# The opening of an encoder kernel, arranged by quarters of the channels

## The chip, the cores and the metric

The kernel runs on one core of a Trainium2 chip. The metric is the device time of one execution in microseconds, the median of several runs. The core has five engines with a queue each: TensorE (PE, with its weight loads as PEld), VectorE (DVE), ScalarE (ACT), GpSimd (POOL) and SyncE (SP), which here issues nearly all DMA transfers.

## What is computed

A two-layer encoder (1024 channels) runs over two sequences: a prompt of 256 tokens and a sample of 512. Each layer normalizes, scales and shifts by a vector that depends on the sequence, mixes the tokens (layer 0 by a gated recurrence in both directions, layer 1 by windowed attention), and then runs a feed-forward part with a short convolution. The change lies in the first microseconds of layer 0:

```python
mod = jax.nn.silu(c) @ adaln_w[l] + adaln_b[l]            # 1024 x 6144
sh1, sc1, g1, sh2, sc2, g2 = jnp.split(mod, 6, axis=-1)
h = rmsnorm(x, norm_g[l, 0]) * (1 + sc1) + sh1
proj = h @ w_in                                           # queries, keys, values, o, gates
q, k, v, o = ...
gates = proj[..., 4096:] + b_gate                         # input and forget gate, both directions
b = cumsum(log_sigmoid(forget)); m = running max(input - b)
```

The gates feed scans over time (cumulative sums and running maxima), whose results weigh the products of queries and keys.

## The kernel before

**Layout.** Channels lie on the 128 partitions, in KC = 8 blocks (called channels c = 0 to 7 here), tokens along the free dimension: 768 columns, the prompt at 0 to 255 and the sample at 256 to 767. RANGES names the sample's first half (r0), its second half (r1) and the prompt (r2). Products run in a split form: an operand is its rounded high part plus a low part (`hh` and `hl` for activations, `whi` and `wlo` for weights), and a product is three matmuls: high by high, high by low, low by high. One *tile* of a projection is 128 output columns by all eight channels, so 24 matmuls for the sample and 24 for the prompt.

**The opening.** `first` (L1728) loads x by ranges and starts `adaln` (L418), which computes shift and scale, the first 2048 columns of the modulation matrix `adaln_w`. It loads sixteen pieces of 128 rows by 1024 columns (512 KB each, the last in two halves), in the order of the rows, and multiplies each by the activated condition `silc` (32 columns, two in use) into four column groups of one PSUM bank. A result is complete only when the last row block is in. Then ACT and DVE copy the bank, PE turns it by 128-column blocks, and DVE adds the bias and forms the gains (1 + scale) * g. Between the loads the helper `warm` (L414) issues plain fp32 matmuls of ones. The two sample ranges are normalized meanwhile (`Norm`, L91: squares on ACT, sums on POOL and PE, a power on POOL, a spread of the factor over partitions on PE), and `scaled` multiplies x by the factor.

`mlstm` (L665) then loads the first two weight halves (`U_MIN`, the queries of head 0), the prompt's x and the rest of the constants, and calls `opening` (L908). There the order of PE, ACT and DVE is written out by hand (`manual_schedule`). Three tiles run: the gates, and the two halves of the queries of head 0. r0 is modulated channel by channel (`made`, `cast`, `lower`) and multiplied, then r1, then the prompt, whose factor comes from a `Norm` of its own. `ahead` (L300) loads and splits the next weight, the first tile of the keys (`U_MIN + 1`, half 0), and is noted as `opened`. The three sinks take the results away.

**Behind it.** The fourth tile, the first of the keys, runs in the loop at L754, then the second, then the values (`gemmN`). `decay` (L696) forms the logarithms and scans on DVE, writes the running maxima to DRAM (L713), and `maxima` (L727) reads them back, spread over partitions. `columns` turns the gates. The rest of the modulation is filled in later: `adaln_g` on PE, `adaln_v` on DVE (one reduction over 1024 columns per vector, L539), the first of them behind `opened`.

**What sets the order.** Outside hand-ordered blocks a list scheduler orders each engine's instructions by a simulated time; on the chip every queue runs in that order. Buffers come from pools with a fixed number of slots: six `slab`, five `raw` (loads of 512 KB), three each of `whi` and `wlo`, four PSUM banks each of `ps` and `pa`. A load waits on SP until its slot is free.

Of the kernel before, what the change touches and what calls it, by code (L numbers as in the profile page):

```python
# [11 lines left out]
F32 = mybir.dt.float32  # L12
# [4 lines left out]
P = 128  # L17
D = 1024
# [33 lines left out]
SOON = AB + 96  # L52
# [129 lines left out]
class Net:  # L182
# [235 lines left out]
    def adaln(self, l, th):  # L418
        nc = self.nc
        hold = None  # L420

        def fetch(i):
            nonlocal hold
            k, h = divmod(i, 2)
            c0 = th * 2048 + h * 1024
            src = self.io["adaln_w"][l, k * P : (k + 1) * P, c0 : c0 + 1024]
            if k < 2:
                return self.raw(src)
            z = (i - 4) % 3
            if z == 0:  # L430
                hold = self.slab([P, 3, 1024])
            for part in parts(i):
                cut = lambda a: a.rearrange("p (g m) -> p g m", g=2)[:, :, part] if len(parts(i)) > 1 else a
                nc.sync.dma_start(cut(hold[:, z]), cut(src))
            return hold[:, z]

        def parts(i):
            return [slice(0, 256), slice(256, 512)] if i == 2 * KC - 1 else [slice(0, 512)]

        ps, pt = self.ps(), self.ps()  # L440
        for i in range(2 * KC):
            k, h = divmod(i, 2)
            cur = fetch(i)
            for part in parts(i):
                for g in range(2):
                    r0 = 32 * (2 * h + g)
                    last = nc.tensor.matmul(
                        ps[r0 : r0 + 32, part], self.silc[:, k, :], cur[:, g * 512 : (g + 1) * 512][:, part],
                        start=k == 0, stop=k == KC - 1, skip_group_check=True,
                    )  # L450
            if h and k > 2:
                with self.tc.issue_after(last.ins):
                    self.warm(pt, 6 if k < KC - 2 else 2 if k < KC - 1 else 1)
            if i < 2 * KC - 1 and h:
                yield
        sb = [self.tmp([P, 256]) for _ in range(2)]
        nc.vector.tensor_copy(sb[0], ps[:, :256])
        nc.scalar.copy(sb[1], ps[:, 256:])
        for b in range(4):
            self.turned = nc.tensor.transpose(  # L460
                pt[:, b * P : (b + 1) * P], sb[b // 2][:, (b % 2) * P : (b % 2 + 1) * P], self.ident
            )
        src = pt.rearrange("p (b g s) -> p g b s", b=4, g=4)[:, :, :, 0:2]
        dst = self.mod[l][:, th * 16 : (th + 1) * 16, :].rearrange("p (g b) s -> p g b s", g=4)
        ab = self.cst(AB + 48 * l + 16 * th, 16).rearrange("p (g b) -> p g b", g=4)
        for s in range(2):
            nc.vector.tensor_tensor(dst[:, :, :, s], src[:, :, :, s], ab, ALU.add)
            if th == 0:
                nc.vector.scalar_tensor_tensor(
                    self.gain[l][0][:, :, s],  # L470
                    self.mod[l][:, 8:16, s],
                    1.0,
                    self.cst(NG + 16 * l, 8),
                    ALU.add,
                    ALU.mult,
                )
        yield

# [42 lines left out]
    def adaln_v(self, columns, pool):  # L521
# [4 lines left out]
        nc.sync.dma_start(row, self.crow.to_broadcast([P, 2, 1024]))  # L526
# [41 lines left out]

    def scaled(self, x, pr, rng):
        for c in range(KC):  # L570
            self.nc.vector.tensor_tensor(x(c), x(c), pr, ALU.mult)
        return ()
# [92 lines left out]
    def mlstm(self, pool, gw, xt):  # L665
# [8 lines left out]
        nc.vector.memset(B[0:G], 0.0)  # L674
# [16 lines left out]
        nc.sync.dma_start(self.kct[:, P:], io["kc"][:, P : 3 * P])  # L691
        nc.sync.dma_start(self.cstt[:, SOON:], io["cst"][:, SOON:])
        self.opening(xt, gw, raws, (gates, keep(qt0, 0, 0), keep(qt0, 0, 1)))
# [53 lines left out]
        for h in range(4):  # L747
# [5 lines left out]
            qk = [] if h else [qt0]  # L753
            todo = ((i, c, w) for i in range(0 if h else 1, 2) for c, w in self.halves(U_MIN + 3 * h + i))  # L754
# [153 lines left out]
    def opening(self, xt, gw, raws, sinks):  # L908

        nc = self.nc  # L910
# [3 lines left out]
        hi, lo = ([self.stg.tile([P, 1024], R, tag=t, name=self.nm(t), bufs=3) for _ in range(2)] for t in ("whi", "wlo"))  # L914
        w = [[t.rearrange("p (k m) -> p k m", k=KC) for t in part] for part in ([gw[0], *hi], [gw[1], *lo])]
        low = lambda i: tt(lo[i], raws[i], hi[i].bitcast(F32), ALU.subtract)
        high = lambda i: nc.scalar.copy(hi[i], raws[i])
# [3 lines left out]
        def mm(rng, i, z, a, c, stop=False):  # L921
            c0, c1, q = rng
            s0 = SEQS[q][0]
            o = bank[i, q][:, c0 - s0 : c1 - s0]
            self.mm(o, w[z][i][:, c], both[a][:, c, c0:c1], (i, c0) not in begun, stop)
            begun.add((i, c0))

        def three(rng, i, c):
            for z, a in ((0, 0), (1, 0), (0, 1)):
                mm(rng, i, z, a, c, c == KC - 1 and a == 1)  # L930
# [7 lines left out]
        r0, r1, r2 = RANGES  # L938
# [3 lines left out]
        shift = lambda c, q: self.mod[0][:, c, q : q + 1]  # L942
        gain = lambda c, q: self.gain[0][0][:, c, q : q + 1]

        def sample(rng):
            c0, c1, q = rng
            x = lambda c: xt[c // 4][:, c % 4, c0:c1]
            h = lambda c: self.hh[:, c, c0:c1]

            def made(c):  # L950
                if c % 2:
                    act(x(c), x(c), AF.Identity, scale=gain(c, q), bias=shift(c, q))
                else:
                    nc.vector.tensor_scalar(x(c), x(c), gain(c, q), shift(c, q), ALU.mult, ALU.add)

            cast = lambda c: nc.scalar.copy(h(c), x(c))  # L956
            lower = lambda c: tt(self.hl[:, c, c0:c1], x(c), h(c).bitcast(F32), ALU.subtract)
            return made, cast, lower

        def operands(rng, *between):  # L960
            made, cast, lower = sample(rng)
            made(0)
            made(1)
            made(2)
            cast(0)
            cast(1)
            for c in range(0, KC, 2):
                lower(c)
                if c + 2 < KC:
                    cast(c + 2)  # L970
                lower(c + 1)
                if c + 4 < KC:
                    made(c + 4)
                if c + 2 < KC:
                    made(c + 3)
                    cast(c + 3)
                if c < 2 * len(between):
                    between[c // 2]()

        squares = lambda c0: [norm.square(c) for c in range(c0, c0 + 4)]  # L980

        with self.tc.manual_schedule(engines={eng.PE, eng.Activation, eng.DVE}):
            for i in range(3):
                bank[i, 0] = self.ps()
            with self.tc.issue_after(self.turned.ins):
                self.warm(bank[0, 0], 5)
            high(0)
            operands(r0)
            high(1)
            low(0)  # L990
            low(1)
            squares(0)
            for c in range(0, KC, 2):
                for k in (c, c + 1):
                    three(r0, 0, k)
                for k in (c, c + 1):
                    mm(r0, 1, 0, 0, k)
                    mm(r0, 1, 0, 1, k)
            for c in range(KC):
                mm(r0, 2, 0, 0, c)  # L1000
                mm(r0, 2, 0, 1, c)
            for i in (1, 2):
                for c in range(KC):
                    mm(r0, i, 1, 0, c, c == KC - 1)

            operands(r1, lambda: squares(4))
            for c in range(0, KC, 2):
                if c == 4:
                    next(factor)
                if c == 6:  # L1010
                    next(factor, None)
                for i in range(3):
                    for k in (c, c + 1):
                        three(r1, i, k)
# [4 lines left out]
            def first(c):  # L1019
                t = self.tmp([P, c1 - c0])  # L1020
                stt(t, xt[c // 4][:, c % 4, c0:c1], gain(c, q), got[r2], ALU.mult, ALU.mult)
                act(self.hh[:, c, c0:c1], t, AF.Identity, bias=shift(c, q))
                return t
# [857 lines left out]
```

## Time and profile before

| | us |
|---|---|
| median of 3 runs (lowest to highest) | 1803.8 (1800.6 to 1807.4) |
| the profiled execution | 1803.0 |
| its span, first to last instruction | 1801.0 |
| mean granted TensorE clock over the span | 0.997 |

The profile shows one execution. A line of the timeline or of the chain gives the start and the length in us and then what ran; a line of a group gives the number of instructions, their busy time and the mean length of one in ns, and behind the second bar the idle time of the engine ahead of them and what ended it. The start of the next matmul, not the modelled end, tells what a matmul costs PE. The lines that matter stand in the prediction.

### The profile page before, as it was taken

Reading aid. Unit: us, or ns where it says so; the run is one execution under the profiler, and the core shown is the slowest. Engines: PE = TensorE matmul, PEld = TensorE weight load, DVE = VectorE, ACT = ScalarE, POOL = GpSimd, SP = SyncE. Lnnn points to the kernel's source line nnn. Section 1 sums busy time; section 2 is a strip of 40 time slices with the busy share of each in tenths; the row PEclk is TensorE's granted clock in tenths of the full one; section 3 lists DMA queues with packets and bytes.
Section 4 is the critical chain, followed back from the end, with each engine's and each line's share of the span. In section 5 each row is a group of like instructions: output and inputs, shape, how many; then the busy total and the mean of one; then the engine's idle time right before and its main releaser. Section 6 shows DMA issues by size and latency. Waiting matters only on the chain.

```text
span 1801.0 us, 28821 instructions
## 1 busy us (share of the span) xinstructions
PE 1763.2 (98%) x11140; PEld 1640.9 (91%) x11140; DVE 1390.2 (77%) x2196; ACT 898.3 (50%) x1822; POOL 511.8 (28%) x433
## 2 busy tenths in 40 slices
PE   7999999999999999999999999999999999999998
PEld 4989878989998999999999999989989999999998
DVE  4887677994899777777777867767998777777877
ACT  4545434443574444444444657665564444444443
POOL 3102010231134233333331314320244333333323
PEclk9999999999999999999999999999999999999999
DMA  9354656555212222222222321233122222222212
GB/s 359 100 168 150 202 191 221 169 180 195 80 50 71 71 70 61 69 71 71 71 71 84 110 89 45 60 101 128 47 82 71 71 71 71 71 71 71 71 36 71
DMA packets 64996, 185.07 MB, mean 103 GB/s; under 512 B 6247, under 2 KB 24839, under 8 KB 64732
## 3 DMA queue, kind: packets, MB, share of 16 engines
q1 hardware_dynamic: 64284, 182.72, 31.8%
q8 instruction: 87, 1.43, 0.3%
q10 hardware_dynamic: 576, 0.52, 0.1%
q14 instruction: 49, 0.40, 0.1%
HBM read 176.77 MB, written 6.44 MB: 102 GB/s over the span
## 4 chain that ended last, share of the span: by engine, by line
PE 84%; DVE 5%; DMA 5%; ACT 3%; issue 2%; POOL 1%; SPq 0%; POOLq 0%; DVEq 0%; ACTq 0%
PE ps L269 26%; PE pa L269 23%; PE ps L1358 11%; PE ps L1359 10%; PE ps L1361 10%; DMA raw<-in_adaln_t_dram 2%; DVE junk L539 1%; DMA raw<-in_w_dram 1%; PE pa L1197 1%; DMA slab<-in_adaln_w_dram 1%; DMA raw<-in_adaln_w_dram 1%; DVE wlo L276 1%; PE pa L1359 0%; PE pa L1358 0%; ACT whi L275 0%
## 5 line engine op out<-in xcount | busy, mean ns | idle before, releaser
L275 ACT CAST whi<-raw 128x1024 fp32r<-128x1024 f32 (+1 forms) x231 | 241.0, 1045 | 342.9 <-PE pa L269 143.8
L276 DVE TENSOR_TENSOR wlo<-raw,whi 128x1024 fp32r<-128x1024 f32 (+1 forms) x231 | 315.9, 1369 | 118.2 <-ACT whi L275 115.8
L269 PE MATMUL pa<-slab,whi 128*128 128x256 f32 (+1 forms) x1280 | 307.6, 335 | 0.0
L269 PEld LDWEIGHTS pa<-slab,whi 128*128 128x128 f32 x1280 | 222.2, 188 | 21.6 <-DVE slab L603 0.4
L603 DVE SCALAR_TENSOR_TENSOR slab<-pa,mod,slab 128x256 f32<-128x256 f32 (+1 forms) x320 | 187.2, 603 | 61.5 <-PE pa L269 61.3
L269 PE MATMUL pa<-slab,wlo 128*128 128x512 f32 (+1 forms) x640 | 205.7, 334 | 0.0
L269 PE MATMUL ps<-zh,whi 128*128 128x256 f32 (+1 forms) x560 | 187.6, 336 | 0.3 <-ACT zh L956 0.3
L269 PE MATMUL ps<-zl,whi 128*128 128x256 f32 (+1 forms) x560 | 183.9, 331 | 0.5 <-DVE zl L564 0.5
L269 PE MATMUL ps<-zh,wlo 128*128 128x256 f32 (+1 forms) x560 | 181.4, 329 | 0.2 <-DVE wlo L276 0.2
L1358 PE MATMUL ps<-zh,whi 128*128 128x384 f32 x504 | 172.5, 342 | 3.8 <-ACT nt L1429 1.9
L269 PE MATMUL ps<-slab,whi 128*128 128x384 f32 (+2 forms) x704 | 172.0, 329 | 0.9 <-DVE slab L276 0.5
L539 DVE CUSTOM_DVE_ANT_0 junk<-raw,crow,cstt 128x1024 f32<-128x1024 f32 x112 | 148.6, 1327 | 30.5 <-DMA raw<-in_adaln_t_dram 29.7
L1359 PE MATMUL ps<-zl,whi 128*128 128x384 f32 x504 | 169.9, 337 | 0.8 <-DVE zl L1315 0.8
L1361 PE MATMUL ps<-zh,wlo 128*128 128x384 f32 x504 | 169.2, 336 | 0.0
L1394 POOL TENSOR_TENSOR raw<-raw,raw 128x512 f32<-128x512 f32 x40 | 53.9, 1348 | 318.4 <-DVE wlo L276 245.6
L1610 POOL TENSOR_TENSOR slab<-slab 128x772 f32<-128x772 f32 x44 | 86.6, 1969 | 166.9 <-DVE slab L1598 149.2
L269 PEld LDWEIGHTS pa<-slab,wlo 128*128 128x128 f32 x640 | 120.4, 188 | 13.2 <-DVE wlo L276 0.4
L1597 DVE SCALAR_TENSOR_TENSOR slab<-slab,cstt,slab 128x771 f32<-128x771 f32 x88 | 105.2, 1198 | 26.5 <-ACT slab L1595 26.3
L269 PEld LDWEIGHTS ps<-slab,whi 128*128 128x128 f32 x704 | 122.5, 188 | 3.4 <-ACT whi L275 0.9
L269 PEld LDWEIGHTS ps<-zh,whi 128*128 128x128 f32 x560 | 106.5, 190 | 13.1 <-issue 3.9
L269 PEld LDWEIGHTS ps<-zl,whi 128*128 128x128 f32 x560 | 106.4, 190 | 9.6 <-DVE zl L564 0.7
L269 PE MATMUL ps<-slab,wlo 128*128 128x384 f32 (+2 forms) x352 | 114.8, 328 | 0.1
(304 smaller groups left out, 4293.3 us busy)
## 6 DMA issues: line engine op xcount, KB each, us to landing
raw<-in_w_dram SPq DMA_DIRECT2D x208, 512.0 KB, 3.8
raw<-in_adaln_t_dram SPq DMA_DIRECT2D x56, 512.0 KB, 4.4
raw<-in_adaln_w_dram SPq DMA_DIRECT2D x28, 512.0 KB, 3.9
slab<-in_x_dram SPq DMA_DIRECT2D x12, 512.0 KB, 8.8
slab<-in_adaln_w_dram SPq DMA_DIRECT2D x11, 512.0 KB, 9.2
slab<-mrows SPq DMA_DIRECT2D x8, 384.0 KB, 6.9
xs<-slab SPq DMA_DIRECT2D x6, 512.0 KB, 3.1
bt<-brow SPq DMA_DIRECT2D x16, 192.0 KB, 3.1
```

What stands on the lines that cost most here:

```text
L269: self.nc.tensor.matmul(out, lhsT, rhs, start=start, stop=stop)
L275: nc.scalar.copy(hi, src)
L276: return nc.vector.tensor_tensor(lo, src, hi.bitcast(F32), ALU.subtract)
L539: nc.vector.tensor_tensor_reduce(out=junk, in0=w, in1=row[:, s], scale=1.0, scalar=self.cst(AB + 48 * l + j), op0=ALU.mult, op1=ALU.add, a ...
L603: return self.nc.vector.scalar_tensor_tensor(x, o, self.mod[l][:, gc + c, q : q + 1], x, ALU.mult, ALU.add)
L1197: nc.tensor.transpose(pp[:, ks], b.t[:, e, ks], self.ident)
L1358: mm(o, wh[:, k], hi[k], start=start and k == 0, stop=False, skip_group_check=True)
L1359: mm(o, wh[:, k], lo[k], start=False, stop=False, skip_group_check=True)
L1361: mm(o, wl[:, k], hi[k], start=False, stop=k == 3, skip_group_check=True)
L1394: tt(q[0], q[2], q[0], ALU.subtract)
L1597: stt(y[:, 1:], u[:, :-1], w(0), y[:, 1:], ALU.mult, ALU.add)
L1610: nc.gpsimd.tensor_tensor(y, y, yrow[:, j], ALU.mult)
```

## The change

The matrix's first 2048 columns are packed anew on the host, by quarters: quarter i holds the shift and scale columns of channels 2i and 2i + 1, for all 1024 rows, in four pieces of 512 KB. `adaln`, `scaled` and the memset of B on DVE are gone; `opening` holds the whole of it, with SP's loads in a written order too. Per quarter there are four modulation steps (`modulation`, 4 matmuls of 256 columns in four column groups), a copy (`out`), a turn by two matmuls with a selecting matrix of 4 columns (`turn`), and `factors`. Then two channels of the sample, all 512 columns at once, are scaled and shifted, and their products follow. Scaling by the norm's factor is now part of that operation, so x isn't multiplied ahead. The sums of squares go channel by channel to PE (`total`), not over POOL. A fourth tile, the first half of the keys, joins the opening: for the sample ahead of the prompt, for the prompt behind the other three. `ahead` now prepares the second half of the keys.

```diff
@@ mlstm
-        nc.vector.memset(B[0:G], 0.0)
...
-        qt0 = self.slab([P, 2, 2, T], R)
-        raws = [self.load(U_MIN, h) for h in range(2)]
-        self.load_x(io["x"], RANGES[2:], xt)
...
+        qt0, kt0 = (self.slab([P, 2, 2, T], R) for _ in range(2))
+        self.opening(pool, (gates, keep(qt0, 0, 0), keep(qt0, 0, 1), keep(kt0, 1, 0)))
+        with self.tc.issue_after(self.opened.ins):
+            nc.gpsimd.memset(B[0:G], 0.0)
...
+                todo = iter([(1, 1, self.early.pop((U_MIN + 1, 1)))])
@@ adaln_v
-        nc.sync.dma_start(row, self.crow.to_broadcast([P, 2, 1024]))
+        with self.tc.issue_after(self.loaded.ins):
+            nc.sync.dma_start(row, self.crow.to_broadcast([P, 2, 1024]))
@@ opening
+        def fetch(i):
+            for j in range(4):
+                n = 4 * i + j
+                t = hold[n // 3][:, n % 3] if n < 12 else raw().rearrange("p (k m) -> p k m", k=2)
+                nc.sync.dma_start(t, io["adaln_h"][i, :, 2 * j : 2 * j + 2])
+                rows.append(t)
+
+        with self.tc.manual_schedule(engines={eng.SP}):
+            xt = self.load_x(io["x"], RANGES[:2])
+            fetch(0)
+            narrow = raw()[:, : 16 * KC]
+            nc.sync.dma_start(narrow, io["wg"])
+            raws = [self.load(U_MIN, h) for h in range(2)]
+            for i in range(1, 4):
+                fetch(i)
+            self.load_x(io["x"], RANGES[2:], xt)
+            keys = self.load(U_MIN + 1, 0)
...
+        def total(rng, cs):
+            for c in cs:
...
+                for b in range(2):
+                    nc.tensor.matmul(
+                        half[rng][:, 2 * b : 2 * b + 2], half[rng, c][:, b * P : (b + 1) * P], self.inv, ...
+        def modulation(i, js):
+            for j in js:
+                for z in range(2):
+                    for g in range(2):
+                        r = 32 * (2 * z + g)
+                        nc.tensor.matmul(
+                            sums[r : r + 32, :256], self.silc[:, 2 * j + z, :], rows[4 * i + j][:, z, 256 * g : 256 * g + 256], ...
+        def out(i):
+            sides[i] = [self.tmp([P, P]) for _ in range(2)]
+            nc.vector.tensor_copy(sides[i][0], sums[:, :P])
+            nc.scalar.copy(sides[i][1], sums[:, P : 2 * P])
+        def turn(i):
+            for b in range(2):
+                nc.tensor.matmul(turned[:, 8 * i + 4 * b : 8 * i + 4 * b + 4], sides[i][b], self.cst(SEL, 4), start=True, stop=True)
...
+        def scaled(c):
+            stt(x(c)[:, S0:S1], x(c)[:, S0:S1], gain(c, 0), pr, ALU.mult, ALU.mult)
+            act(self.hh[:, c, S0:S1], x(c)[:, S0:S1], AF.Identity, bias=shift(c, 0))
+        def lower(c):
+            stt(self.hl[:, c, S0:S1], x(c)[:, S0:S1], shift(c, 0), self.hh[:, c, S0:S1].bitcast(F32), ALU.add, ALU.subtract)
...
+            squares(r0, range(KC))
+            total(r0, range(KC))
+            power(r0)
+            squares(r1, range(KC))
+            modulation(0, (0,))
+            spread(r0)
+            total(r1, range(4))
+            modulation(0, (1,))
+            total(r1, range(4, KC))
+            power(r1)
+            modulation(0, (2,))
+            spread(r1)
+            self.warm(spare, 4)
+            modulation(0, (3,))
+            out(0)
+            self.warm(spare, 4)
+            turn(0)
...
+            factors(0)
+            cast(1)
+            scaled(0)
+            scaled(1)
+            lower(0)
+            rest(1)
+            lower(1)
+            cast(2)
+            rest(2)
+            self.warm(spare, 14)
+            sample(0, 0)
+            sample(0, 1)
+            modulation(1, (0,))
...
+            modulation(1, (2,))
+            self.warm(spare, 4)
+            modulation(1, (3,))
+            out(1)
+            self.warm(spare, 4)
+            turn(1)
+            factors(1)
+            for c in (2, 3):
+                scaled(c)
+            for c in (2, 3):
+                lower(c)
+            modulation(2, (0,))
+            self.warm(spare, 8)
+            modulation(2, (1,))
+            for i in range(3):
+                sample(i, 2)
+            modulation(2, (2,))
+            sample(0, 3)
+            modulation(2, (3,))
+            out(2)
+            sample(1, 3)
+            sample(2, 3)
+            turn(2)
...
+            modulation(3, (0,))
+            modulation(3, (1,))
+            for i in range(3):
+                sample(i, 4)
+            modulation(3, (2,))
+            sample(0, 5)
+            modulation(3, (3,))
+            out(3)
+            sample(1, 5)
+            sample(2, 5)
+            turn(3)
+            factors(3)
+            for c in range(4):
+                norm.square(c)
+            for c in (6, 7):
+                scaled(c)
...
+            self.warm(spare, 8)
+            for c in (6, 7):
                 for i in range(3):
+                    sample(i, c)
+            next(factor)
+            for c in range(4):
+                sample(3, c)
+            next(factor, None)
+            for c in range(4, KC):
+                sample(3, c)
...
+                for i in range(3):
+                    prompt(i, c)
...
             for c in range(KC):
+                prompt(3, c)
+            self.opened = self.ahead(U_MIN + 1, 1)
+            sinks[3](0, bank[3, 0])
```

Here `sample(i, c)` is the three matmuls of 512 columns of tile i and channel c, `prompt(i, c)` the same over 256 columns; `cast(i)` and `rest(i)` split weight i on ACT and DVE.

More of the change, by code (lines that the diff above doesn't have):

```diff
@@ L416, in warm @@
             self.mm(o[:, :P], self.ones, self.ones, True, True)
[L418 to L477, printed above, removed]
@@ L752, in mlstm @@
                 mb = soon
[L753 to L754 removed]
+            qk = [] if h else [qt0, kt0]
+            if h:
+                todo = ((i, c, w) for i in range(2) for c, w in self.halves(U_MIN + 3 * h + i))
+            else:
+                todo = iter([(1, 1, self.early.pop((U_MIN + 1, 1)))])
             now = next(todo)
@@ L913, in opening @@
         eng = mybir.EngineType
[L914 to L917, printed above, removed]
+        r0, r1, r2 = RANGES
+        S0, S1 = SEQS[0]
+        x = lambda c: xt[c // 4][:, c % 4]
@@ new lines, in opening @@
+        hold = [self.slab([P, 3, 2, 512]) for _ in range(4)]
+        raw = lambda: self.stg.tile([P, 1024], F32, tag="raw", name=self.nm("raw"), bufs=5)
+        rows = []
+        def fetch(i):
[14 more added lines that the diff above has]
+            keys = self.load(U_MIN + 1, 0)
+            nc.sync.dma_start(self.kct[:, P:], io["kc"][:, P : 3 * P])
+            self.loaded = nc.sync.dma_start(self.cstt[:, SOON:], io["cst"][:, SOON:])
@@ new lines, in opening, with weight @@
+        hi, lo = ([self.stg.tile([P, 1024], R, tag=t, name=self.nm(t), bufs=3) for _ in range(3)] for t in ("whi", "wlo"))
+        for t in hi[0], lo[0]:
+            nc.gpsimd.memset(t.bitcast(F32), 0.0)
+        cut = lambda t: t.rearrange("p (k m) -> p k m", m=P)
+        kw = [[cut(pool.tile([P, n], R, tag="PT", name=self.nm("PT"), bufs=8)) for n in (640, 384)] for _ in range(2)]
+        def weight(z, i, c):
+            if i == 3:
+                return kw[z][c // 5][:, c % 5]
+            return cut((hi, lo)[z][i])[:, c]
@@ L928, in three, with sample, prompt @@
-        def three(rng, i, c):
-            for z, a in ((0, 0), (1, 0), (0, 1)):
-                mm(rng, i, z, a, c, c == KC - 1 and a == 1)
+            o = bank[i, q][:, t0 - s0 : t1 - s0]
+            self.mm(o, weight(z, i, c), both[a][:, c, t0:t1], (i, q) not in begun, stop)
+            begun.add((i, q))
+        def sample(i, c, *za):
+            for z, a in za or ((0, 0), (1, 0), (0, 1)):
+                mm(z, i, a, c, S0, S1, 0, c == KC - 1 and (z, a) == (0, 1))
+        def prompt(i, c):
+            for z, a in ((0, 0), (1, 0), (0, 1)):
+                mm(z, i, a, c, 0, S0, 1, c == KC - 1 and a == 1)
@@ new lines, in opening, with squares @@
+        shift = lambda c, q: self.mod[0][:, c, q : q + 1]
+        gain = lambda c, q: self.gain[0][0][:, c, q : q + 1]
+        pr = self.pa()
+        sums = self.pa()
+        turned = self.pa()
+        half = {}
+        def squares(rng, cs):
+            for c in cs:
+                sq = self.tmp([P, 256])
+                act(sq, x(c)[:, rng[0] : rng[1]], AF.Square)
+                half[rng, c] = sq
+        def total(rng, cs):
+            for c in cs:
+                if c == 0:
+                    half[rng] = self.pa()
+                for b in range(2):
+                    nc.tensor.matmul(
+                        half[rng][:, 2 * b : 2 * b + 2], half[rng, c][:, b * P : (b + 1) * P], self.inv,
+                        start=c == b == 0, stop=c == KC - 1, skip_group_check=True,
+                    )
@@ L941, in opening @@
         next(factor)
[L942 to L958, printed above, removed]
```

165 lines of the change are left out of this document (73 added, 92 removed).

## The prediction

> **What bounds the kernel now.** First the page: busy times and the chain of work that ended last.
>
> ```profile
> PE 1763.2 (98%) x11140; PEld 1640.9 (91%) x11140; DVE 1390.2 (77%) x2196; ACT 898.3 (50%) x1822; POOL 511.8 (28%) x433
> PE 84%; DVE 5%; DMA 5%; ACT 3%; issue 2%; POOL 1%; SPq 0%; POOLq 0%; DVEq 0%; ACTq 0%
> ```
>
> TensorE is the bound, and the 5% of DMA lies mostly where the change is. So the question is when TensorE's useful work begins, and what else it has to do. Next the chain over the first 40 us (start, us, what):
>
> ```profile
> 14.83 8.44 DMA slab<-in_adaln_w_dram
> 23.29 9.51 DMA slab<-in_adaln_w_dram
> ...
> 32.85 0.65 PE ps L447 x4
> ```
>
> The modulation matrix ends its landing at 32.80; its last matmuls, the turn and the first operands follow. The timeline of PE gives two marks: the first product, and the end of the keys' first tile, the fourth of all (the matmul at 73.11 opens the next one).
>
> ```profile
> 36.37 0.38 PE L269 MATMUL ps<-zh,whi 128*128 128x256 f32 x1 [0.28 <-ACT zh L956]
> ...
> 73.11 0.40 PE L269 MATMUL ps<-zh,whi 128*128 128x512 f32 x1
> ```
>
> Both kernels have done the same four tiles at the mark that is 73.1 here, and the PE work behind it is the same. So I look for when that mark comes after the change.
>
> **The change, part by part.** Loads first: windows of 10 us (last column GB/s), and from the timeline an early store on SP and the first squares.
>
> ```profile
> 0.00:10.00 10.00, 0.94 (x4) 0.22 (x4) 0.46 (x4) 5.62 (x12) 4.81 (x10) 1.00 0.71 244
> 10.00:20.00 10.00, 9.60 (x56) 3.94 (x53) 3.86 (x10) 0.47 (x2) 1.56 (x3) 1.00 1.04 399
> 4.47 0.33 SPq L390 DMA_DIRECT2D crows<-crow  x1
> 6.19 2.64 ACT L112 ACTIVATE nt<-slab 128x256 f32<-128x256 f32 x8 [1.75 <-DMA slab<-in_x_dram]
> ```
>
> A piece of 512 KB (0.524 MB) takes 1.3 us at 400 GB/s, and the first one is there at 6.2. In the new order x fills four pieces (6.2, 7.5, 8.8, 10.1) and the quarters' pieces start to land at 11.4. Quarter 0 is there by 15.3, the weights by 18, quarter 1 by 23, quarter 2 by 28, quarter 3 by 33.5, the prompt by 36 and the keys by 37.5. The new order has the bytes early; that is the point of it. What it costs is PE's time, since every step now stands in one written order on PE. The prices on PE, by start to start: a product of 512 and of 256 columns, the two-column sums, the warming matmuls, and the modulation by 256 columns as the later groups do it (16 records are two steps).
>
> ```profile
> 68.22 0.39 PE L269 MATMUL ps<-zh,wlo 128*128 128x512 f32 x1
> ...
> 70.03 0.39 PE L269 MATMUL ps<-zl,whi 128*128 128x512 f32 x1
> ...
> 70.59 0.28 PE L269 MATMUL ps<-zh,whi 128*128 128x256 f32 x1
> 70.71 0.28 PE L269 MATMUL ps<-zl,whi 128*128 128x256 f32 x1
> ...
> 24.30 1.60 PE L269 MATMUL ps<-ones 128*128 128x128 f32 x12
> 25.74 1.40 PE L269 MATMUL pa<-inv,nt 128*128 128x2 f32 x12
> ...
> 129.34 0.28 PE L269 MATMUL ps<-zh,wlo 128*128 128x256 f32 x1
> 129.55 1.07 PE L269 MATMUL ps<-raw,silc 128*32 128x256 f32 x16
> 130.55 0.50 PE L269 MATMUL ps<-zh,whi 128*128 128x512 f32 x1
> ```
>
> The rows at 68.22 and 70.03 are eight products apart: 0.227 us for 512 columns, and 0.12 for 256. A plain fp32 matmul is two records 0.11 apart: the twelve "ones" are six calls of the helper, 0.22 each, and a two-column sum is 0.22 as well. For two modulation steps PE gives 130.55 - 129.34 - 0.12 = 1.09 us, of which about 0.2 is the change between narrow and full matmuls; a step alone is then 0.44 + 0.2 = 0.64. The new turn (two fp32 matmuls by 4 columns) isn't in the trace; its nearest row is the two-column sum, so 0.45 for two.
>
> *First product.* PE sums the first range's squares as they come: 16 sums, 3.6 us, done by 10.2. The first modulation step waits for its piece, 11.4. From there PE is full: four steps 2.6, two spreads 1.2, 16 sums of the second range 3.6, a wait of 0.6 for the power on POOL, eight warming calls 1.8, the turn 0.45, fourteen warming calls 3.1. That is 13.3, so the first product is at **24.6**, 11.8 earlier than 36.4. These warming calls hide the way from the turn to the first operand, which the following rows price:
>
> ```profile
> 33.59 0.42 DVE L457 COPY nt<-ps 128x256 f32<-128x256 f32 x1 [0.70 <-PE ps L447]
> 35.00 0.26 DVE L467 TENSOR_TENSOR mod<-ps,cstt 128x16 f32<-128x16 f32 x2 [0.99 <-PE ps L460]
> L828 DVE TENSOR_TENSOR E<-pa,E 128x512 f32<-128x512 f32 x1 | 0.7, 677 | 0.0
> L1022 ACT ACTIVATE zh<-nt,mod 128x256 fp32r<-128x256 f32 x8 | 3.8, 505 | 5.9 <-DVE nt L1021 5.9
> L1031 DVE SCALAR_TENSOR_TENSOR zl<-nt,mod,zh 128x256 fp32r<-128x256 f32 x8 | 3.8, 480 | 1.0 <-ACT zh L1022 1.0
> ```
>
> Factors are three small DVE operations, 0.5 with the wait; scaling 512 columns is 0.7 on DVE; the high part on ACT 0.5 plus another 256 columns, so 0.72; the low part, in the same way, 0.75. About 2.0 us lie between a turn and the first high part, and 0.75 more before its low part. At every quarter something must fill that: modulation steps and warming calls do.
>
> *From the first product to the mark*, on PE: 96 sample products of 512 columns, 96 x 0.227 = 21.8; 96 prompt products, 96 x 0.12 = 11.5; the prompt's sums and spread 1.05; together 34.4, which the old kernel does too (36.4 to 73.1 is 36.7, with halves of 256 columns, 0.9 dearer, and 1.5 of small waits). New between them: twelve modulation steps 7.7, 24 warming calls (4+4+8+8) 5.3, three turns 1.35. Waits that stay, by the latencies above: 0.6 for the low part of channel 1, behind the split of the first weight on DVE; 0.9 + 0.4 at channel 4, where only two modulation steps (1.3) stand against 2.2; 0.4 + 0.4 at channel 6. Sum: 24.6 + 34.4 + 7.7 + 5.3 + 1.35 + 2.6 = **75.9** against 73.1. The 11.8 us that the early start wins are spent on 14.4 us that used to lie under the DMA.
>
> The other edits cost nothing. The zeroing of B (2.6 on DVE) goes to POOL, whose cover is that the scan which reads it comes 10 us behind the opening's end. The fourth tile's split stands on ACT and DVE beside products of channels 6 and 7 (4.1 us against 2.4). The last two pieces of quarter 3 and the keys wait on SP for buffers that the splits at 21 to 27 us free, while seven loads are in flight.
>
> **Bounds.** If modulation steps overlap fully with their neighbours (0.43) and no wait stays: 70.9, a gain of 2.2. The upper end is the clock. The groups of PE's matmuls before 12.2 us and after 13.7:
>
> ```profile
> L447 PE MATMUL ps<-raw,silc 128*32 128x512 f32 x8 | 3.2, 1058 | 9.1 <-DMA raw<-in_adaln_w_dram 9.1
> L447 PE MATMUL ps<-raw,silc 128*32 128x512 f32 x8 | 1.1, 604 | 0.0
> ```
>
> The same matmul is nearly twice as long at first, so the array starts slow, and is fast about 3.5 us after its first matmul at 9.06. After the change the first matmuls come at 6.6, and they are sums of two columns. With slow work until 10 to 13.6, as here, the waits absorb part and the mark moves by 0.7 to 1.7; with slow work until 25 it is 81.4. I take one more microsecond for the clock and one less for modulation steps that stand in pairs: the mark comes **3 us later**.
>
> The Trainium skill (TensorE: Matmul & The Clock Gate, Part 1: The HAM clock gate) says that the array runs at half rate until about 3.4 us of sustained activity release it. The rows agree with the ratio and the time; whether two-column sums count as activity no run here shows, and if they don't, the 81.4 above is what follows.
>
> **Behind the mark.** The gates feed the scans on DVE, whose maxima go out through DRAM and are read back:
>
> ```profile
> 63.79 0.46 ACT L678 ACTIVATE slab<-pa,cstt 36x256 f32<-36x256 f32 x1
> 88.24 0.36 SPq L713 DMA_DIRECT2D mrows<-slab  x1
> 90.34 1.76 SPq L730 DMA_DIRECT2D slab<-mrows  x4
> slab<-mrows SPq DMA_DIRECT2D x6, 384.0 KB, 6.6
> 107.62 1.13 DVE L815 SCALAR_TENSOR_TENSOR E<-slab,aT,kct 128x128 f32<-128x128 f32 x4
> ```
>
> The maxima are there at 90.3 + 6.6 = 97 and are used at 107.6: 10.6 us to spare. After the change the prompt's gates end 2.9 before the mark, at 73, not 63.8: 9.5 later. The maxima then land at 106.5, and the use moves with PE to about 110.5. Four microseconds stay; I charge nothing.
>
> So the profiled execution, 1803.0 us with a span of 1801.0, would become 1806; the median of the runs shown, 1803.8, becomes **1807**.
>
> **Rivals.**
> *The clock (slower).* If two-column sums don't wake the array, all of PE's opening runs slow to 25 us: mark 81.4, +8.3, and the maxima are 8 later too; with a microsecond of that exposed, 1813. It decides if the first 128-column warming calls run at 0.43 each. For it: the sparse work up to 16 us. Against it: sums still load 128-column weights and are back to back.
> *The gates' chain (slower).* If DVE puts the column reductions (1.28 each) ahead of the scans, four of them use up the spare 4 us and each further one is lost: 1809 to 1813. For it: DVE has 17 of them between 62 and 125. Against: they start only behind the opening, so fewer can be ahead.
> *Load order (the change not as it says).* If SP issues the store of crow's rows, which waits for ACT until 4.47, ahead of x, everything lands 2.3 later, and so does the mark: 1809. Against it: here x, there at 6.2, was issued ahead of that store, and nothing in the diff puts the store first.
> *Better packing (faster).* Mark at 70.9, and the order behind it happens to lose this wait and the slow clock behind it:
>
> ```profile
> 189.08 1.07 PE L269 MATMUL ps<-raw,silc 128*32 128x256 f32 x16 [1.83 <-DMA raw<-in_adaln_w_dram]
> 190.00:195.00 5.00, 5.00 (x23) 4.15 (x20) 1.29 (x2) 0.00 (x0) 0.00 (x0) 0.66 1.00 378
> ```
>
> That is 1.8 and a third of 5 us: 1803.8 - 2.2 - 3.5 = 1798. For it: this stretch is decided by load times that shift. Against: the steps stand singly between products, where the narrow and full matmuls must change over.
>
> **How the numbers follow.** Forecast 55% (1803 to 1810), better packing 17% (1796 to 1803), load order 7%, gates' chain 10%, clock 11%. The range leaves out the lower half of the packing case and the far end of the clock's: 1799 to 1813. A measurement of this kernel tells about 0.5% (9 us) from no change: faster by more needs the whole packing case and 4 us besides, 0.06; slower by more, most of the clock's and part of the chain's case, 0.14; within, 0.80.
>
> **What would show it.** The first product near 24.6 (slow clock: beyond 30); PE without gaps over 1 us from there on; the first product of the keys' second tile at 75 to 77; warming calls at 0.22; the high part of channel 2 ready before PE has done its eight warming calls, so that these are lost; the maxima landing a few microseconds ahead of their use. I am wrong if modulation steps cost under 0.45 between products, or if PE after the mark has fewer stalls than now.

## The result, and the profile after

| | before | after |
|---|---|---|
| median (lowest to highest), 4 runs each | 1802.2 (1800.1 to 1807.4) | 1815.1 (1813.2 to 1816.6) |
| ratio to before, 95% interval | | 1.0067 [1.0042, 1.0091] |
| profiled execution, its span | 1803.0, 1801.0 | 1814.8, 1813.0 |
| first product (profiled execution) | 36.4 | 33.0 |
| the mark (the keys' second tile opens; profiled execution) | 73.1 | 87.8 |

The changed kernel is 12.8 us slower, outside the range that I gave. The first product comes 3.4 us earlier instead of 11.8, and the mark 14.7 later instead of 3. On the page, the busy times and the engines' shares of the chain that ended last:

```profile
PE 1779.3 (98%) x11220; PEld 1653.8 (91%) x11220; DVE 1379.6 (76%) x2183; ACT 895.3 (49%) x1810; POOL 508.6 (28%) x424
PE 83%; DVE 7%; DMA 4%; ACT 3%; issue 2%; POOL 1%; SPq 0%; POOLq 0%; DVEq 0%; ACTq 0%
```

PE is busy 16.1 us longer (1763.2 before) with 80 matmuls more: the DMA's share has fallen by a point, and PE has more than that to do. The timeline of PE in the opening of the changed kernel shows where:

```profile
6.79 6.99 PE L927 MATMUL pa<-inv,nt 128*128 128x2 f32 x32 [6.79 <-ACT nt L919]
13.70 1.08 PE L948 MATMUL pa<-slab,silc 128*32 128x256 f32 x8
14.80 1.22 PE L270 MATMUL pa<-kct,nr 128*128 128x128 f32 x4
15.82 3.41 PE L927 MATMUL pa<-inv,nt 128*128 128x2 f32 x16
19.16 1.08 PE L948 MATMUL pa<-slab,silc 128*32 128x256 f32 x8
20.17 3.58 PE L927 MATMUL pa<-inv,nt 128*128 128x2 f32 x16
...
25.79 1.91 PE L270 MATMUL ps<-ones 128*128 128x128 f32 x8
27.64 0.90 PE L948 MATMUL pa<-slab,silc 128*32 128x256 f32 x8
28.47 1.16 PE L270 MATMUL ps<-ones 128*128 128x128 f32 x8
...
32.96 0.48 PE L270 MATMUL ps<-zh,whi 128*128 128x512 f32 x1
```

From 6.8 on PE has hardly a gap, but until 28.2 everything takes about twice its price. The 16 records at 15.82 last until the next row, 19.16: 0.21 each, where the prediction's row had 0.11. A modulation step takes 1.01 (19.16 to 20.17). The eight "ones" at 25.79 go at 0.23, those at 28.47 at 0.12. In the trace's clock records the full clock begins at 28.23 us (12.64 before). The window view doesn't tell this:

```profile
0.00:28.00 28.00, 21.17 (x108) 18.17 (x112) 0.78 (x6) 8.59 (x20) 3.44 (x8) 1.00 0.92 349
```

The third number from the end, the granted clock, says 1.00 because no record exists before the first release. Ahead of that point the spacing of starts is the clock to read.

Behind the first product, three places of PE's timeline: the wait at channel 4, a wait in the prompt's loop, the mark.

```profile
54.34 0.50 PE L270 MATMUL ps<-zh,whi 128*128 128x512 f32 x1 [0.99 <-ACT zh L975]
...
81.83 0.39 PE L270 MATMUL pa<-zl,whi 128*128 128x256 f32 x1 [0.91 <-DVE zl L1120]
...
87.80 0.40 PE L270 MATMUL ps<-zh,whi 128*128 128x512 f32 x1
```

Of the 14.7 us at the mark 12.8 are left in the time. The values start at 81.45 before and at 96.12 after. The 200 us from there on, as windows (before, then after; the first busy time is PE's):

```profile
81.40:281.40 200.00, 191.68 (x1374) 168.96 (x1377) 147.16 (x300) 88.80 (x232) 24.34 (x34) 0.99 0.55 180
```

```profile
96.10:296.10 200.00, 195.03 (x1412) 172.15 (x1411) 155.58 (x315) 91.13 (x240) 27.06 (x35) 1.00 0.56 186
```

PE is busy 3.35 us more of the 200, at a clock that doesn't fall: the wait of 1.83 and the slow stretch at 190 that the prediction quotes are not met in this form. From the values to the start of PE's last matmul it is 1710.5 us, against 1713.4 before.

### The profile page after: what moved, and what is told of

The parts are those of the page before. It is cut to its first block, busy times and chain, and to the rows that moved or that the text cites. A ratio compares the mean times of both kernels' runs of the same rounds, so it can differ in the third digit from the quotient of the medians.

```text
span 1813.0 us, 28950 instructions
## 1 busy us (share of the span) xinstructions
PE 1779.3 (98%) x11220; PEld 1653.8 (91%) x11220; DVE 1379.6 (76%) x2183; ACT 895.3 (49%) x1810; POOL 508.6 (28%) x424
## 4 chain that ended last, share of the span: by engine, by line
PE 83%; DVE 7%; DMA 4%; ACT 3%; issue 2%; POOL 1%; SPq 0%; POOLq 0%; DVEq 0%; ACTq 0%
PE ps L270 25%; PE pa L270 23%; PE ps L1447 10%; PE ps L1448 10%; PE ps L1450 10%; DMA raw<-in_adaln_t_dram 2%; DVE junk L480 2%; DMA raw<-in_w_dram 2%; PE pa L1286 1%; PE pa L927 1%; DVE wlo L277 1%; ACT whi L276 1%; PE pa L948 1%; PE pa L1447 0%; PE pa L1448 0%
## 5 line engine op out<-in xcount | busy, mean ns | idle before, releaser
L276 ACT CAST whi<-raw 128x1024 fp32r<-128x1024 f32 x229 | 239.7, 1048 | 341.1 <-PE pa L270 144.2
L277 DVE TENSOR_TENSOR wlo<-raw,whi 128x1024 fp32r<-128x1024 f32 x229 | 312.1, 1364 | 121.6 <-ACT whi L276 119.2
L270 PE MATMUL ps<-zh,whi 128*128 128x256 f32 (+1 forms) x520 | 178.9, 344 | 1.1 <-ACT zh L975 1.0
L270 PE MATMUL ps<-zl,whi 128*128 128x256 f32 (+1 forms) x520 | 174.1, 336 | 0.8 <-DVE zl L505 0.5
L270 PE MATMUL ps<-zh,wlo 128*128 128x256 f32 (+1 forms) x520 | 173.0, 335 | 0.3 <-DVE wlo L277 0.3
L1686 DVE SCALAR_TENSOR_TENSOR slab<-slab,cstt,slab 128x771 f32<-128x771 f32 x88 | 103.8, 1181 | 26.6 <-ACT slab L1684 26.4
L270 PEld LDWEIGHTS ps<-zh,whi 128*128 128x128 f32 x520 | 98.4, 189 | 17.3 <-issue 6.0
L1687 DVE SCALAR_TENSOR_TENSOR slab<-slab,cstt,slab 128x771 f32<-128x771 f32 x88 | 110.2, 1252 | 0.8
```

The costliest lines, as they stand in the source:

```text
L270: self.nc.tensor.matmul(out, lhsT, rhs, start=start, stop=stop)
L276: nc.scalar.copy(hi, src)
L277: return nc.vector.tensor_tensor(lo, src, hi.bitcast(F32), ALU.subtract)
L1686: stt(y[:, 1:], u[:, :-1], w(0), y[:, 1:], ALU.mult, ALU.add)
L1687: stt(y[:, :-1], u[:, 1:], w(2), y[:, :-1], ALU.mult, ALU.add)
```

## The experiments

**The theories.** The *clock theory*: the two-column sums don't count as work for the clock gate, so the opening runs at half clock until 28 us; the rest is roughly as forecast. The *order theory*: whatever the clock, PE's written order holds steps, warming calls and waits that used to lie under the DMA. No kernel leaves out a part of the computation. Times are medians, and ratios are against runs of the kernel before in the same group (1802.8, 1803.2 and 1803.0 us in the three groups of experiments); "first" and "mark" are PE's starts as above, each from one profiled execution.

| kernel | first | mark | time | ratio [95%] |
|---|---|---|---|---|
| the change | 32.96 | 87.80 | 1815.1 | 1.0067 [1.0042, 1.0091] |
| e1_wake | 30.74 | 85.60 | 1811.4 | 1.0054 [1.0040, 1.0068] |
| e2_wake_no_fill | 28.45 | 85.29 | 1811.8 | 1.0053 [1.0041, 1.0066] |
| e3_wake_steps_twice | 32.24 | 91.58 | 1820.7 | 1.0105 [1.0091, 1.0118] |
| e4_reorder | 28.26 | 75.68 | 1801.9 | 0.9999 [0.9991, 1.0008] |
| f1_wide_sums | 26.93 | 81.85 | 1808.8 | 1.0031 [1.0020, 1.0041] |
| f2_wake_wide_sums | 24.96 | 79.83 | 1805.6 | 1.0016 [1.0006, 1.0027] |
| f3_reorder_wide_sums | 22.42 | 69.89 | 1796.9 | 0.9964 [0.9952, 0.9977] |
| f4_late_sinks | 33.39 | 87.47 | 1815.4 | 1.0068 [1.0054, 1.0081] |
| g1_pool_sums | 29.05 | 83.89 | 1810.9 | 1.0043 [1.0030, 1.0057] |
| g2_three_tiles | 22.01 | 74.50 | 1800.5 | 0.9985 [0.9974, 0.9996] |
| g3_tuned | 20.62 | 67.35 | 1793.1 | 0.9948 [0.9934, 0.9961] |

**Wake the array first (e1_wake).** Thirteen warming calls while x is on its way:

```diff
             spare = bank[3, 0]
+            self.warm(spare, 13)
             squares(r0, range(KC))
```

> The changed kernel with one line more: thirteen plain fp32 matmuls of ones on PE from the moment the ones exist (1 us) until the first squares come (6.5 us). Theory A (the array stays at half clock until 28 us because two-column sums and sparse modulation steps do not wake it): full clock by 8 us, two-column sums 0.11 apart and not 0.21, first product at 24.6 to 26 (33.0 in the changed kernel), end of the fourth tile at 78 to 80 (87.8), time 7 to 9 us below the changed kernel. Theory B (the sums and steps are paced by ACT, DMA or waits, and the clock is only a by-product): full clock earlier, but the first product still beyond 30 and the time within 2 us of the changed kernel.

The timeline of PE, then two windows of the same kernel (granted clock third from the end):

```profile
1.05 5.21 PE L270 MATMUL ps<-ones 128*128 128x128 f32 x26 [1.05 <-DVE inv L379]
6.50 4.95 PE L927 MATMUL pa<-inv,nt 128*128 128x2 f32 x32 [0.25 <-ACT nt L919]
11.75 1.08 PE L948 MATMUL pa<-slab,silc 128*32 128x256 f32 x8 [0.29 <-DVE nr L935]
...
30.74 0.48 PE L270 MATMUL ps<-zh,whi 128*128 128x512 f32 x1
```

```profile
5.50:8.50 3.00, 2.75 (x25) 2.56 (x24) 0.00 (x0) 2.46 (x8) 0.00 (x0) 1.00 1.05 360
9.00:25.50 16.50, 16.19 (x84) 13.47 (x84) 0.32 (x2) 2.72 (x8) 1.40 (x2) 0.50 1.03 409
```

The calls wake the array at 5.36, and it goes back to half clock at 8.77, in the middle of the sums, with PE busy nearly all the while; it stays there until 25.84. So waking alone brings the first product 2.2 us earlier, not eight. That the sums fail to wake the array was only half of it: a woken array also falls back while they run.

**No warming calls behind that (e2_wake_no_fill).** e1 without the seven later groups (46 calls):

```diff
-            self.warm(spare, 4)
...
-            self.warm(spare, 14)
...
-            self.warm(spare, 8)
```

> e1_wake without the seven later groups of warming calls (46 calls). Theory A, second half (each call takes 0.22 us of PE, and those that outlast the wait they cover are lost): the end of the fourth tile 2.5 to 3.5 us ahead of e1_wake, time 2 to 3.5 us below it, gaps of up to 2.2 us on PE behind the first and the last turn. Rival: the gaps let the clock fall to half again, for 3.4 us or more, and the time is that of e1_wake or above.

```profile
25.44 1.01 PE L962 MATMUL pa<-cstt,nt 128*128 128x4 f32 x4 [0.49 <-DVE nt L957]
28.45 0.80 PE L270 MATMUL ps<-zh,whi 128*128 128x512 f32 x1 [1.99 <-ACT zh L975]
29.04 0.63 PE L270 MATMUL ps<-zh,wlo 128*128 128x512 f32 x1
29.46 0.63 PE L270 MATMUL ps<-zl,whi 128*128 128x512 f32 x1
```

The first product comes 2.3 us earlier, and PE waits 1.99 us for its operand (second row, in brackets). But the products then start 0.42 apart: the clock stays at half until 36.47, and falls once more from 60.36 to 63.77. The mark moves by 0.3, the time not at all. The calls cost PE about what they save in clock; real work in their place is what could win.

**Every later step twice (e3_wake_steps_twice).** e1, with each modulation step of quarters 1 to 3 issued a second time into a spare bank:

```diff
+                if i:
+                    for z in range(2):
+                        for g in range(2):
+                            r = 32 * (2 * z + g)
+                            nc.tensor.matmul(spare[r : r + 32, :256], self.silc[:, 2 * j + z, :], ...
```

> e1_wake with each of the twelve modulation steps of quarters 1 to 3 issued twice, the second time into a bank whose content is thrown away. If a step costs PE its 0.43 us and is on the path: 12 x 0.43 = 5.2 us more than e1_wake, less some 1 us where it takes the place of a wait. If PE waits anyway: under 1 us more.

The mark moves 6.0 us against e1, the time 9.3. Of the 6.0, 1.5 lie ahead of the first product, where no step was added: there the half clock lasted until 28.29 rather than 25.84. The other 4.5 are 0.37 for each of twelve steps, so these stand fully on the path (a second step behind the first shares its change of form). Behind the mark another 3.3 appear that the marks don't explain.

**Real work as filler (e4_reorder).** e1, with half of a quarter's products held back behind the next turn in place of warming calls (26 calls are left, 13 of them early), the weights' casts behind the first operands, and the results of the queries taken away behind the prompt's loop:

```diff
-                if i == 1:
-                    modulation(1, (1,))
...
-            modulation(1, (2,))
-            self.warm(spare, 4)
-            modulation(1, (3,))
+            modulation(1, (2, 3))
             out(1)
-            self.warm(spare, 4)
+            for c in (0, 1):
+                sample(1, c, *pl)
             turn(1)
+            for c in (0, 1):
+                sample(2, c, *pl)
+            modulation(2, (0, 1))
```

> The same parts in another order, with the early matmuls of e1_wake: the second half of each quarter's products stands behind the next quarter's turn in place of warming calls (13 + 13 calls in all), the first quarter's steps follow each other as they land, the weights' splits stand behind the first operands, and the query results leave behind the prompt's loop. By the prices of the trace: first product at 20, first operand of channels 6 and 7 at 42, end of the fourth tile at 63 to 66 (73.1 before the change), time 6 to 10 us below the kernel before. If instead the load of the last matrix piece or of the keys sets the pace: end of the fourth tile at 69 or later.

The half clock is still there (8.35 to 25.42), and the first product comes at 28.3, not 20, the mark at 75.7, not 63 to 66. From the one to the other it is 47.4 us against 54.8 of the change: 7.4 us of the order theory's kind. The time is that of the kernel before. Both theories have a part.

**Wide sums (f1_wide_sums, f2_wake_wide_sums).** The sums of squares against a matrix of 128 ones in place of two columns of 1/1024, with the division in the operation behind: the same number of matmuls, of the same length at full clock, with 64 times the columns. f2 adds e1's early calls.

```diff
-                        half[rng][:, 2 * b : 2 * b + 2], half[rng, c][:, b * P : (b + 1) * P], self.inv,
+                        half[rng][:, P * b : P * b + P], half[rng, c][:, b * P : (b + 1) * P], self.ones,
...
-            nc.vector.tensor_scalar(r, mean, EPS, None, ALU.add)
+            nc.vector.tensor_scalar(r, mean, 1.0 / D, EPS, ALU.mult, ALU.add)
```

> The changed kernel with one thing changed: the sums of squares are taken with the 128x128 ones in place of the two columns of 1/D (the division moves into the operation that adds epsilon). As many matmuls, and a pass over 128 columns is as long as one over two (0.11 us at full clock). Theory A1 (two-column matmuls do not count as activity, so the array stays or falls to half clock while the sums run, as the wake-up of e1_wake ended one window later): full clock within 7 us of the first sum, by 14 us, the first product at 25 to 28 (33.0), end of the fourth tile at 80 to 83 (87.8), time 5 to 8 us below the changed kernel's 1815.1. Rival A2 (any matmuls so sparse in time leave the clock down, whatever their width): clock and time as in the changed kernel.

> f1_wide_sums with the thirteen early matmuls of e1_wake. A1: the clock is full from 5 to 9 us on and stays so, first product at 24.5 to 26, end of the fourth tile at 79 to 80.5, time 1806 to 1807.5. A2: clock falls back after one window as in e1_wake, time as e1_wake (1811.4).

PE's timeline of f1, with sums that stand where the narrow ones stood:

```profile
6.60 6.63 PE L927 MATMUL pa<-ones,nt 128*128 128x128 f32 x32 [6.60 <-ACT nt L919]
13.15 0.64 PE L948 MATMUL pa<-slab,silc 128*32 128x256 f32 x8
14.26 0.71 PE L270 MATMUL pa<-kct,nr 128*128 128x128 f32 x4 [0.46 <-POOL nr L936]
14.80 1.95 PE L927 MATMUL pa<-ones,nt 128*128 128x128 f32 x16
...
26.93 0.48 PE L270 MATMUL ps<-zh,whi 128*128 128x512 f32 x1
```

The clock is full from 12.47 on, the second range's 16 records take 1.9 us instead of 3.4, and the first product is 6.0 earlier. That is the clock theory, shown by one operand. In f2 the clock is full from 5.52 through the whole opening:

```profile
6.74 3.84 PE L927 MATMUL pa<-ones,nt 128*128 128x128 f32 x32 [0.40 <-ACT nt L919]
11.72 0.64 PE L948 MATMUL pa<-slab,silc 128*32 128x256 f32 x8 [1.14 <-DMA slab<-in_adaln_h_dram]
...
24.96 0.48 PE L270 MATMUL ps<-zh,whi 128*128 128x512 f32 x1
```

The same early calls that won 2.2 us in e1 hold here: the first product is at 24.96, the forecast's 24.6 but for 0.4. Yet the kernel is still slower than before, 2.9 us [1.1, 4.9], by the order alone.

**Sums on POOL again (g1_pool_sums).** The change with the squares of channels 0 to 5 added on POOL, as before, so that 24 of the 64 records of narrow sums are left on PE:

```diff
+                if 0 < c < 6:
+                    nc.gpsimd.tensor_tensor(half[rng, 0], half[rng, 0], sq, ALU.add)
...
+                if 0 < c < 6:
+                    continue
```

> The changed kernel with one part undone: channels 0 to 5 of the squares are added on POOL again and PE sums three results per range, as before the change. A1 (two-column matmuls keep the array slow, and there are now 24 records of them and not 64): the first modulation steps wake the array as in the kernel before, full clock at 15 to 20 us, first product at 25 to 28 (33.0), end of the fourth tile 5 to 8 us earlier (87.8), time 1807 to 1810. Rival: the steps land 1.3 us apart and are too sparse as well, the clock comes after 24 us, and the gain is under 3 us.

```profile
11.49 2.72 PE L931 MATMUL pa<-inv,nt 128*128 128x2 f32 x12 [11.49 <-POOL nt L922]
14.14 1.08 PE L952 MATMUL pa<-slab,silc 128*32 128x256 f32 x8
...
17.06 1.08 PE L952 MATMUL pa<-slab,silc 128*32 128x256 f32 x8
...
19.87 1.08 PE L952 MATMUL pa<-slab,silc 128*32 128x256 f32 x8
...
23.83 0.80 PE L952 MATMUL pa<-slab,silc 128*32 128x256 f32 x8
```

With few sums the array still wakes only at 24.22: modulation steps every 3 to 4 us, with narrow sums and spreads between them, don't wake it either. The first product and the mark are 3.9 us earlier, with a full clock that comes 4.0 earlier; how much of this is PE's smaller work at half clock isn't told apart. So taking most of the narrow sums away isn't enough: there must be enough wide work.

**Results later (f4_late_sinks).** The change with the queries' two results taken away behind the prompt's loop rather than in it:

```diff
-                if c in (3, 5):
-                    sinks[c // 2](0, bank[c // 2, 0])
...
-            sinks[3](0, bank[3, 0])
+            for i in (1, 2, 3):
+                sinks[i](0, bank[i, 0])
```

> The changed kernel, where the sample's two query results leave behind the prompt's loop and not inside it. If their ACT and DVE work inside the loop delays the prompt's operands: the loop's 72 products take 8.7 us and not 10.4, end of the fourth tile 1.7 us earlier, time 1 to 2 us below the changed kernel. Rival: the second keys tile then waits for the bank or for the weight's split, and the gain is gone behind the loop.

```profile
87.47 0.50 PE L270 MATMUL ps<-zh,whi 128*128 128x512 f32 x1 [0.61 <-DVE slab L280]
```

The loop falls from 10.2 to 8.6 us, start to start. But the next tile needs a bank that one of the moved results still holds (the 0.61 in the row), and the clock came 1.3 us later in this execution, the first product 0.4. The mark gains 0.3 of 1.6 and the time nothing. A wait was moved, not removed.

**Order and wide sums together (f3), without the fourth tile (g2), and tuned (g3).** f3 is e4 with wide sums. g2 is f3 with the keys' first tile back behind the opening. g3 is f3 with two shifts:

```diff
-            modulation(0, (0,))
             total(r1, range(4))
-            spread(r0)
+            modulation(0, (0,))
             total(r1, range(4, KC))
+            spread(r0)
...
+            sinks[1](0, bank[1, 0])
             self.opened = self.ahead(U_MIN + 1, 1)
-            for i in (1, 2, 3):
+            for i in (2, 3):
```

> e4_reorder with the wide sums. A1: full clock throughout, first product at 20 to 22 (28.3), end of the fourth tile 6 to 8 us ahead of e4_reorder, at 67 to 69 (75.4), where the load of the last matrix piece may take back some; time 6 to 8 us below e4_reorder and the kernel before: 1794 to 1797. A2: as e4_reorder.

> f3_reorder_wide_sums with the fourth tile taken out of the opening and run behind it, as before the change (the prompt's factor is then waited for on PE). If the fourth tile is there to cover the prompt's sums, power and first operand: PE waits 2.5 to 3.5 us ahead of the prompt, and the time is that much above f3 (1799 to 1800). If it covers nothing: within 1 us of f3.

> f3_reorder_wide_sums with half of the second range's sums ahead of the first modulation step (PE waits there 1.6 us for the load) and the first query result taken away ahead of the last weight's split (the second keys tile waits 0.6 us for its bank). By the sum of the two waits, first product 1.5 us earlier, end of the fourth tile 2 us earlier, time 1.5 to 2 us below f3: 1795. If the loads take the pace up again at quarters 2 and 3: first product earlier, fourth tile the same, time within 0.7 us of f3.

f3 is 0.36% [0.23, 0.48] faster than the kernel before, within its forecast; its first product and its mark are 0.4 and 0.9 us later than forecast. Without the fourth tile PE waits for the prompt's norm where f3 has products; PE's timeline of g2:

```profile
51.59 0.71 PE L270 MATMUL pa<-kct,nr 128*128 128x128 f32 x4 [1.03 <-POOL nr L163]
53.47 0.58 PE L270 MATMUL pa<-zh,whi 128*128 128x256 f32 x1 [1.17 <-ACT zh L1079]
```

Two waits, 2.2 us together, and the half clock from 52.63 to 59.46 behind them: the mark is 4.6 later than f3's and the ratio 0.0021 higher, some 4 us across two groups of runs. In this order the fourth tile ahead of the prompt is worth those 4 us; how much of that is the half clock isn't told apart. g3 is the best version: from the sums to the first product PE's timeline shows no wait over a quarter of a microsecond,

```profile
6.57 5.63 PE L927 MATMUL pa<-ones,nt 128*128 128x128 f32 x48 [0.24 <-ACT nt L919]
12.12 0.64 PE L948 MATMUL pa<-slab,silc 128*32 128x256 f32 x8
...
20.62 0.50 PE L270 MATMUL ps<-zh,whi 128*128 128x512 f32 x1
```

and its time is 1793.1 us, 0.52% [0.39, 0.66] below the kernel before. Against f3 its first product is 1.8 us earlier and its mark 2.5, somewhat more than the sum of the two waits; the ratio is 0.0016 lower, about 3 us across two groups of runs. Across two groups as well, it is 22 us below the change.

## Why the prediction was wrong

**The failed step is the clock.** I took "one more microsecond for the clock" and had the first product at 24.6. It came at 32.96, 8.4 us later, and 8.0 of these go with the clock: the first product of f2 is at 24.96. At the mark f2 is 8.0 earlier too (79.83), so this term alone is nearly two thirds of the result. The error was to let slow work end at 10 to 13.6, as in the kernel before, where matmuls of 512 columns ran. f2 differs from the change only in the columns of its sums and the early calls; so the loads, the four steps, the sums, the fill and the latency of the first operand were priced right as a sum.

**The clock rival was the mechanism, and its price too low.** I gave it 11%, a mark of 81.4 and 1813. Its test, the first warming calls at 0.43 each, came true (two records at 0.23). It assumed slow work until 25, which made 5.5 us at the mark (81.4 less 75.9); the steps are sparse as well (g1), the clock came at 28.2, and the cost was 8.0. My argument against it, that sums "still load 128-column weights and are back to back", is what the runs refute. The Trainium skill (TensorE: Matmul & The Clock Gate, Part 1: The HAM clock gate) has the throttle released by sustained activity over a window of 3.4 us and set again after an idle one. The time agrees: e1 falls back 3.41 us after its release. But from 5.5 to 8.5, inside that window, PE was 2.75 of 3.00 us busy by e1's first window row; so "activity" can't be read as a busy queue here. f1 shows that the number of columns matters; how much the gate asks for, no run here tells.

**From the first product to the mark 54.8 us, not 51.3.** f2 has 54.9, so this isn't the clock. Two terms of the sum were mis-sized. *The prompt's loop*: 72 products at 0.12 are 8.6, measured 10.2 (74.71 to 84.93). I had not counted that the queries' results are taken away inside it. PE's rows for both terms, then ACT and DVE inside the loop, of the changed kernel:

```profile
36.67 0.64 PE L948 MATMUL pa<-slab,silc 128*32 128x256 f32 x8
37.24 0.50 PE L270 MATMUL ps<-zh,whi 128*128 128x512 f32 x1
...
39.28 0.64 PE L948 MATMUL pa<-slab,silc 128*32 128x256 f32 x8
...
74.71 0.28 PE L270 MATMUL pa<-zh,whi 128*128 128x256 f32 x1
...
84.93 0.40 PE L270 MATMUL ps<-zh,PT 128*128 128x256 f32 x2
```

```profile
80.08 0.58 ACT L279 ACTIVATE slab<-ps 128x512 fp32r<-128x512 f32 x1
80.69 0.69 DVE L280 SCALAR_TENSOR_TENSOR slab<-ps,slab 128x512 fp32r<-128x512 f32 x1 [1.06 <-ACT slab L279]
81.30 0.48 DVE L1120 SCALAR_TENSOR_TENSOR zl<-nt,mod,zh 128x256 fp32r<-128x256 f32 x1
```

DVE idles 1.06 us behind the copy on ACT, then takes the result, and only then forms the low part for which PE waits 0.91 at 81.83. f4 confirms the size (1.6). *The modulation steps*: I had 0.64 for a single one, with the change of form in it. From its start to the next product it is 0.57 (36.67 to 37.24), but the eight products behind it take 2.04 us (to 39.28), 0.22 more than 8 x 0.227; so a single step costs about 0.78. Ten of them are 1.4 us. The two terms are 3.0 of the 3.5; where the other 0.5 lies isn't shown.

**What held.** The load order: the last piece of quarter 0 is there before its turn on PE, and only one of the four early pieces of x was issued behind crow's store, so that rival didn't come. The early start is spent on work that used to lie under the DMA: with the clock full (f2) 11.4 us are won at the first product and the mark is still 6.7 later than before. Behind the mark, nothing was to be charged: the maxima are issued at 112.73, landed 5.0 us later and are used at 119.56, 1.8 to spare where I had four, and PE's only wait from there to 126 us is 0.17, at 125.56. The gates' chain didn't bind. The better packing's second half, stalls lost behind the mark, did come in part (2.9 us between the values and PE's end, in the two profiled executions), which I had counted on only in that rival.

**The sum.** Clock 8.0, loop 1.6, steps 1.4 and 0.9 besides make the 11.9 us between my sum's 75.9 and the measured mark. The mark is 14.7 later than before, and 1.9 us are regained behind it: 12.8 slower where I had said 3.2.

**What stays open.** The stretch from the values to PE's end is 1706.8 to 1713.4 us in these kernels, and no run isolates why. One thing that differs is in the clock records: in the kernel before, e4, f2, f3, g1 and g2 the clock falls to half once for 3.41 us, between 187 and 206 us, and the stretch is 1711.3 to 1713.4 us; in the change, e1, e2, e3, f4 and g3 it doesn't, and the stretch is 1706.8 to 1712.3 (f1's clock falls at 1310: 1710.3). With this stays open why e3 lost 3.3 us more than its mark. Whether fewer columns than 128 would do for the sums wasn't tried.

## What to carry to other kernels

A plain fp32 matmul with two columns took as long in PE's queue here as one with 128 (two records of 0.11 us), and did not keep the clock up; where sums are needed in an opening, use the wide form. When steps are moved out from under a wait for DMA, each of them is then PE's time, with what it adds to its neighbours. Fill latencies with products held back for it: warming calls cost about what they save (e2), while an order with held-back products turned the same idea from slower (f2) into faster (f3, g3). That order holds other shifts too, of splits and results, and their shares weren't taken apart.

## What the hardware showed unexpectedly

A busy PE lost its full clock: in e1 at 8.77 us, 3.41 us after the release, in an unbroken run of two-column sums that at full clock start 0.11 us apart. The same run with 128 columns kept it (f2, from 5.52 on). Nor did modulation steps bring the full clock, one every 2.8 to 4 us in g1 (24.22) and every 4 to 5.5 us in the change (28.23). Even products of 512 columns took long: in e2 they start at 28.45, with two modulation steps and a wait of 0.3 between them, and the clock is full only at 36.47. In these traces the clock moves in whole steps of 3.41 us: the half clock lasts 17.07 us in e1 and in e4 (five), 20.48 in e3 (six), 27.31 in e2 (eight). So where such a step ends decides over a microsecond or two: e3's first product is 1.5 later than e1's, with one step more at half clock, and f4, which is the change up to the prompt's loop, got its full clock 1.3 later.
